# A hybrid decoder step on one core: the first norm's squares on ScalarE with a fixed order of additions, and the gMLP masks applied in the rotation tables' buffers

## The chip, the core and the metric

The kernel runs on one NeuronCore of a Trainium2 chip. The core has TensorE (PE in the profile: matrix products from SBUF into PSUM), VectorE (DVE), ScalarE (ACT), GpSimd (POOL) and SyncE (SP, which here only issues DMAs). Each engine works through its own queue in order and waits on semaphores for the others. The metric is the device time of one execution in microseconds; lower is better.

## What is computed

One step of a two-layer decoder for a prompt of 512 tokens and for 64 sample tokens (8 sequences of 8), 576 columns in all, width 1024, in float32. Layer 0 runs retention heads beside a gMLP, layer 1 a sliding-window attention; each is followed by a squared-ReLU MLP. The change is in the first norm and in the gMLP's masks of layer 0:

```python
def rmsnorm(x, g):
    x32 = x.astype(jnp.float32)
    y = x32 * lax.rsqrt(jnp.mean(x32 * x32, axis=-1, keepdims=True) + RMS_EPS)
    return (y * g.astype(jnp.float32)).astype(x.dtype)
...
def mixer_ab(h, pos, s0, w_in, w_s, b_s, ln_g, ln_b, w_o):
    z = h @ w_in
    q, k, v, g, u, gv = jnp.split(z, AB_SPLITS, axis=-1)
    q = rotary(q.reshape(B, L, RET_HEADS, RET_DK), pos)
    k = rotary(k.reshape(B, L, RET_HEADS, RET_DK), pos)
    o, s_new = retention(q, k, v, s0.astype(jnp.float32))
...
    causal = jnp.tril(jnp.ones((GM_CHUNK, GM_CHUNK), dtype=bool))
    w = jnp.where(causal[None], w_s, 0.0).astype(vn.dtype)
    mixed = jnp.einsum('gij,bnjgd->bnigd', w, vc) + b_s.T.astype(vn.dtype)[None, None, :, :, None]
```

`hn = rmsnorm(h, norm_mix[0])` feeds `mixer_ab`; the outputs are both residual streams after the last norm, the retention states, the normalised gMLP rows and the key and value caches.

## The kernel before

**Layout.** Activations lie transposed: eight chunks `h[0..7]` of 128 channels x 576 tokens. A float32 product is made of three fp32r products: an operand x is split into `hi` (rounded to fp32r) and `lo` (the rest), and `block` (line 330) adds hi·hi, hi·lo and lo·hi, in two halves of 288 columns, in PSUM. One chunk of the input projection is thus 8 x 6 = 48 products into an accumulator `acc` (two of them in PSUM). Weights come by DMA into `raw` (three buffers), `whi` is cast on ACT (L278), `wlo` subtracted on DVE (L289), each in a ring of six buffers.

**The norm comes late.** `operands(c)` multiplies h[c] by the gain only: `xhi` on ACT, `xlo` on DVE (L426). The factor rstd (one over the root mean square of a token) is applied to the products when they leave PSUM. So the projection starts before the norm is known. Squares are taken on ACT (L435) or POOL (L433), added on POOL (L441) into `ssq`; `two_parts` (L393) splits ssq, and `mean_rsqrt` (L398) multiplies it by a matrix of 1/1024 on PE (L404, L405), which sums over the channels, then takes a root on ACT (L406) and one Newton step on DVE (L407, L389 to L391).

**The start of `mixer0`** (line 698). For each chunk c: operands, a square, every second time the split of a 256-column piece of weights (`whf`, `wlf`, L227), then 12 products: v of head 0 and k of head 0 grow together in both accumulators, while h still arrives. Then `v1`, the product for v of head 1, in two small PSUM banks (`m_tile`, a ring of four), with the norm's products among it. Then `v_out(0)` frees the first accumulator (`vz`, L809), the rotation tables `cosr` and `sinr` are multiplied by rstd, and `k_out`, `q_out` rotate (`rotary`, line 784: three products on DVE, L786 to L788, and a sum on POOL, L789). Each result is passed on in later slots: `to_tokens` transposes on PE into m_tiles (`tp`, `tq`), `tokens` copies them (ACT) and makes `v2h`, `v2l` (L823) and the masked `vm` (POOL, L827); `scores` multiplies `sc`, `kv`, `scs` and `cx` (L872 to L882), all in m_tiles.

**The gMLP's masks.** The matrices `wst` (128 x 512) and `ws8` (64 x 256) are loaded and multiplied by a triangle on POOL (L1037, L1039) in the code behind the first gv chunk; they are read in `spatial` (L990, L992), after the second gate chunk. Their buffers are their own; cosr and sinr take two of the 21 buffers of the ring `w`.

**Order.** DVE and ACT run as written from line 730 to line 1011, and again in the last chunk and the MLPs (`manual_schedule`). Elsewhere, and on PE, POOL and SP everywhere, a scheduler orders the instructions by its own estimates when the kernel is built; so POOL took up the masks long ahead of their place in the code.

## Time and profile before

| | |
|---|---|
| median of 3 runs | 1206.8 us (1206.55 to 1207.28) |
| the profiled execution's own time | 1204.73 us |
| its span | 1202.9 us |
| instructions on DVE, ACT, POOL | 1691, 1111, 130 |
| share of DVE, ACT, POOL in the span | 76%, 49%, 12% |
| moved by DMA | 109.43 MB, mean 91 GB/s |

The span is the time from the first to the last instruction that the profiler saw; the execution's own time is a little longer. A row of the profile names the line of the code, the engine, the operation, what is written and read (`out<-in`, buffer numbers left out), and how often. In rows in order of time the first two numbers are the start and the length in microseconds (several alike in a row are merged, x2), and a bracket at the end tells how long the engine had been idle before and whom it waited for. DMA issues are SPq.

### The profile page before, as it was taken

To read this page: it belongs to the slowest core of one execution; us is meant where nothing else is said; L and a number is where in the kernel's file an instruction comes from. 1 tells how busy PE (TensorE), PEld (TensorE's weight loads), DVE (VectorE), ACT (ScalarE), POOL (GpSimd) and SP (SyncE) were. 2 spreads that over 40 slices of the span, in tenths; PEclk is the share of its full clock that TensorE was granted. 3 is DMA by queue.
4 is the path that set the end of the run, shared out by engine and by line. 5 is a ranking of instruction groups with operands and counts; after the bars stand their busy time and mean duration, and the time that the engine had idled before them with its cause. 6 is when DMAs were issued, how large, how long until landed. Compare 5 with 4: busy or idle time off the path is not lost.

```text
span 1202.9 us, 22619 instructions
## 1 busy us (share of the span) xinstructions
PE 1182.9 (98%) x9130; PEld 1164.8 (97%) x9130; DVE 908.2 (76%) x1691; ACT 588.4 (49%) x1111; POOL 148.3 (12%) x130
## 2 busy tenths in 40 slices
PE   8999999999999999999999999999999999999996
PEld 8899999999999999999999998999999999999996
DVE  8977797987866876885797787546785795795696
ACT  6333554654534444443466877445453453453452
POOL 4444250000000000000002653220000000000000
PEclk9999999999999999999999999999999999999999
DMA  7343222322332232242223211122233233233322
GB/s 269 110 142 112 88 65 80 88 81 78 90 106 87 77 117 71 71 120 75 88 87 111 72 53 55 53 76 71 84 105 89 71 106 91 68 106 88 87 73 79
DMA packets 38264, 109.43 MB, mean 91 GB/s; under 512 B 4160, under 2 KB 12544, under 8 KB 38144
## 3 DMA queue, kind: packets, MB, share of 16 engines
q1 hardware_dynamic: 37440, 107.36, 29.1%
q8 instruction: 72, 1.18, 0.4%
q10 hardware_dynamic: 720, 0.62, 0.2%
q14 instruction: 32, 0.26, 0.1%
HBM read 102.92 MB, written 6.03 MB: 91 GB/s over the span
## 4 chain that ended last, share of the span: by engine, by line
PE 82%; DVE 10%; ACT 4%; DMA 3%; issue 1%; SPq 0%; DVEq 0%; ACTq 0%
PE acc L334 50%; PE acc L346 10%; PE y L346 4%; PE f L346 4%; PE w L346 3%; PE z L346 3%; DVE wlo L289 3%; DMA raw<-in_w_dn 2%; ACT s L1158 1%; DVE alo L505 1%; PE tpp L1218 1%; DVE h L557 1%; ACT ahi L504 1%; PE dn L334 1%; PE op L1233 1%
## 5 line engine op out<-in xcount | busy, mean ns | idle before, releaser
L334 PE MATMUL acc<-xhi,whi 128*128 128x288 f32 x1504 | 321.7, 295 | 0.3 <-DVE vz L809 0.3
L334 PE MATMUL acc<-xhi,wlo 128*128 128x288 f32 x1504 | 319.2, 293 | 0.0
L334 PE MATMUL acc<-xlo,whi 128*128 128x288 f32 x1504 | 318.6, 293 | 0.0
L289 DVE TENSOR_TENSOR wlo<-raw,whi 128x512 fp32r<-128x512 f32 x317 | 235.7, 757 | 68.8 <-ACT whi L278 67.5
L334 PEld LDWEIGHTS acc<-xhi,whi 128*128 128x128 f32 x1504 | 239.5, 188 | 1.6 <-issue 1.1
L334 PEld LDWEIGHTS acc<-xhi,wlo 128*128 128x128 f32 x1504 | 240.5, 188 | 0.3
L334 PEld LDWEIGHTS acc<-xlo,whi 128*128 128x128 f32 x1504 | 240.1, 188 | 0.0
L278 ACT CAST whi<-raw 128x512 fp32r<-128x512 f32 x317 | 188.9, 619 | 100.5 <-PE acc L334 73.3
L501 ACT ACTIVATE q<-t 128x576 f32<-128x576 f32 x64 | 44.0, 687 | 227.8 <-DVE t L496 227.8
L278 ACT CAST whi<-s 128x512 fp32r<-128x512 f32 x140 | 83.4, 621 | 72.4 <-DVE s L263 62.8
L496 DVE SCALAR_TENSOR_TENSOR t<-acc,rstd 128x576 f32<-128x576 f32 x64 | 48.3, 755 | 80.6 <-PE acc L334 80.4
L289 DVE TENSOR_TENSOR wlo<-s,whi 128x512 fp32r<-128x512 f32 x140 | 95.9, 697 | 10.8 <-ACT whi L278 10.8
L505 DVE TENSOR_TENSOR alo<-q,ahi 128x864 fp32r<-128x864 f32 x64 | 77.2, 1205 | 8.3 <-ACT ahi L504 8.3
L504 ACT CAST ahi<-q 128x864 fp32r<-128x864 f32 x64 | 66.6, 1041 | 13.5 <-DVE q L536 12.5
L346 PE MATMUL acc<-ahi,wlo 128*128 128x288 f32 x340 | 71.4, 298 | 0.6
L346 PE MATMUL acc<-ahi,whi 128*128 128x288 f32 x340 | 71.4, 295 | 0.0
L346 PE MATMUL acc<-alo,whi 128*128 128x288 f32 x340 | 70.4, 295 | 0.0
L1102 POOL TENSOR_TENSOR kl<-z,kh 64x512 fp32r<-64x512 f32 x4 | 5.5, 1374 | 475.1 <-ACT kh L1099 474.9
L263 DVE TENSOR_TENSOR s<-raw 128x512 f32<-128x512 f32 x70 | 48.7, 695 | 19.8 <-DMA raw<-in_w_dn 19.8
L346 PEld LDWEIGHTS acc<-ahi,wlo 128*128 128x128 f32 x340 | 53.5, 188 | 2.5 <-DVE wlo L289 2.5
L346 PEld LDWEIGHTS acc<-ahi,whi 128*128 128x128 f32 x340 | 54.0, 188 | 0.0
L346 PEld LDWEIGHTS acc<-alo,whi 128*128 128x128 f32 x340 | 53.7, 188 | 0.0
(386 smaller groups left out, 2118.8 us busy)
## 6 DMA issues: line engine op xcount, KB each, us to landing
raw<-in_w_up SPq DMA_DIRECT2D x64, 512.0 KB
raw<-in_w_dn SPq DMA_DIRECT2D x64, 512.0 KB
raw<-in_w_in SPq DMA_DIRECT2D x22, 512.0 KB
raw<-in_w_o SPq DMA_DIRECT2D x16, 512.0 KB
raw<-in_w_qkv SPq DMA_DIRECT2D x10, 512.0 KB
h<-in_xT SPq DMA_DIRECT2D x8, 288.0 KB
s<-in_s SPq DMA_DIRECT2D x4, 512.0 KB
out_ret_s<-s SPq DMA_DIRECT2D x4, 512.0 KB
```

The costliest lines, as they stand in the source:

```text
L263: nc.vector.tensor_tensor(out=sums[k, i], in0=x, in1=b[y], op=ALU.add)
L278: nc.scalar.copy(out=hi, in_=src)
L289: nc.vector.tensor_tensor(out=lo, in0=src, in1=hi.bitcast(F32), op=ALU.subtract)
L334: nc.tensor.matmul(out, lhsT=w_, rhs=x_[:, hf if isinstance(hf, slice) else half(hf)], start=(start and si == 0), stop=(stop and si == 2))
L346: nc.tensor.matmul(out, lhsT=w[wi][:, k * P:(k + 1) * P], rhs=x(k)[xi], start=(start and n == 0), stop=(stop and n == len(steps) - 1), ski ...
L496: nc.vector.scalar_tensor_tensor(out=halves(t), in0=view, scalar=0.0, in1=norm.rv, op0=ALU.max, op1=ALU.mult)
L501: nc.scalar.activation(out=flat(q[:, seg]), in_=t, func=AF.Square)
L504: nc.scalar.copy(out=hi[:, s0 - 1:s1 - 1], in_=q[:, s0:s1])
L505: nc.vector.tensor_tensor(out=lo[:, s0 - 1:s1 - 1], in0=q[:, s0:s1], in1=hi.bitcast(F32)[:, s0 - 1:s1 - 1], op=ALU.subtract)
L557: nc.vector.tensor_tensor(out=row[:, cols_], in0=row[:, cols_], in1=src, op=op)
L1158: nc.scalar.activation(out=s[:, n, cut_:], in_=s[:, n, cut_:], func=AF.Exp, bias=nm[:, n:n + 1], accum_out=den[:, n:n + 1])
L1218: nc.tensor.transpose(out=tp[:, i * P:(i + 1) * P], in_=s[:, n, hf * P:(hf + 1) * P], identity=ident)
```

## The change

All eight squares of the first norm are taken on ACT. They are added on DVE in one chain of seven additions into the square of chunk 1, at places that the code writes down (`add`); DVE and ACT run in written order from the first chunk on. The sum isn't split any more: `finish(True)` multiplies it as float32 by `ones_d` (one product for each half instead of two). The split of the first weights is written in another order among this. `ones_v` and `eps_l` are made earlier. cosr and sinr get a pair of buffers of their own (`rot`), which wst and ws8 take over after the last rotation; the ring `w` shrinks from 21 to 19.

```diff
--- before.py
+++ after.py
@@ -35,7 +35,7 @@
 RMS_EPS = 1e-6
 LN_EPS = 1e-5
 MINF = -1e30
-NW = 21
+NW = 19
 NW1 = 26
 NSB = 4
 NK = 9
@@ -397,12 +397,14 @@
 
     def mean_rsqrt(ones_r, sq, out, temp, parts_=None):
 
-        hi, lo = parts_ or two_parts(sq, temp)
+
+        parts_ = parts_ or two_parts(sq, temp)
         r0, x = temp("rs0"), temp("rsx")
         for hf in range(2):
             ms = m_tile("ms")
-            nc.tensor.matmul(ms[:, 0:TH], lhsT=ones_r, rhs=hi[:, half(hf)], start=True, stop=False)
-            nc.tensor.matmul(ms[:, 0:TH], lhsT=ones_r, rhs=lo[:, half(hf)], start=False, stop=True)
+            for n, part in enumerate(parts_):
+                nc.tensor.matmul(ms[:, 0:TH], lhsT=ones_r, rhs=part[:, half(hf)], start=(n == 0),
+                                 stop=(n == len(parts_) - 1))
             nc.scalar.activation(out=r0[:, half(hf)], in_=ms[:, 0:TH], func=AF.Abs_reciprocal_sqrt, bias=eps_r)
             nc.vector.scalar_tensor_tensor(out=x[:, half(hf)], in0=ms[:, 0:TH], scalar=RMS_EPS, in1=r0[:, half(hf)],
                                            op0=ALU.add, op1=ALU.mult)
@@ -427,12 +429,9 @@
                                            op0=ALU.mult, op1=ALU.subtract)
             self.xs.append((hi, lo))
 
-        def square(self, c, pool=False, add=True, eng=None):
+        def square(self, c, add=True, eng=None):
             sq = ks("ssq" if c == 0 else "sq")
-            if pool:
-                nc.gpsimd.tensor_tensor(out=sq, in0=h[c], in1=h[c], op=ALU.mult)
-            else:
-                nc.scalar.activation(out=sq, in_=h[c], func=AF.Square)
+            nc.scalar.activation(out=sq, in_=h[c], func=AF.Square)
             if not add:
                 return sq
             if c == 0:
@@ -440,9 +439,12 @@
             else:
                 (eng or nc.gpsimd).tensor_tensor(out=self.ssq, in0=self.ssq, in1=sq, op=ALU.add)
 
-        def finish(self, parts_=None):
+        def finish(self, plain=False):
             self.rstd = ks("rstd")
-            mean_rsqrt(ones_dr, self.ssq, self.rstd, ks, parts_)
+            if plain:
+                mean_rsqrt(ones_d, self.ssq, self.rstd, ks, [self.ssq])
+            else:
+                mean_rsqrt(ones_dr, self.ssq, self.rstd, ks)
             self.rv = halves(self.rstd)
 
     def add_residual(dc, view, bias=None):
@@ -707,35 +709,51 @@
                 off, wd = C0W[name]
                 return cst[:, off:off + wd]
 
+            ones_v = mp.tile([P, P], F32R, name="ones_v", bufs=1)
+            nc.gpsimd.tensor_scalar(out=ones_v, in0=ones_d, scalar1=float(D // P), scalar2=None, op0=ALU.mult)
+            eps_l = mp.tile([P, 1], F32, name="eps_l", bufs=1)
+            nc.gpsimd.memset(eps_l, LN_EPS)
+
 
             accs = [acc_tile() for _ in range(2)]
-            rest = []
+            inorder = tc.manual_schedule(engines={mybir.EngineType.DVE, mybir.EngineType.Activation})
+            inorder.__enter__()
+            squares = {}
+
+            def square(*chunks):
+                for c in chunks:
+                    squares[c] = norm.square(c, False)
+
+            def add(*chunks):
+                for c in chunks:
+                    nc.vector.tensor_tensor(out=squares[1], in0=squares[1], in1=squares[c], op=ALU.add)
+
             for c in range(KC):
                 norm.operands(c)
-                if c:
-                    rest.append(norm.square(c - 1, c in (1, 3), c <= 5))
+                if c in (4, 6):
+                    square(c - 2)
                 if c % 2 == 0:
                     hi = wp.tile([P, 512], F32R, name="whf", tag="whi", bufs=NW_)
                     lo = wp.tile([P, 512], F32R, name="wlf", tag="wlo", bufs=NW_)
                     split_into(first[c // 2], hi, lo)
+                if c in (1, 3, 5):
+                    square(c // 2 if c < 5 else 3)
+                add(*{4: [0], 5: [2], 6: [3]}.get(c, []))
                 for j in range(2):
                     ws = slice((c % 2) * 256 + j * P, (c % 2) * 256 + (j + 1) * P)
                     block([accs[j][:, hf, 0:TH] for hf in range(2)], (hi[:, ws], lo[:, ws]), norm.xs[c], (0, 1),
                           c == 0, c == KC - 1)
-            sq5, sq6, sq7 = rest[-2], rest[-1], norm.square(KC - 1, False, False)
-            nc.vector.tensor_tensor(out=sq5, in0=sq5, in1=sq6, op=ALU.add)
-            nc.vector.tensor_tensor(out=sq5, in0=sq5, in1=sq7, op=ALU.add)
-
-            inorder = tc.manual_schedule(engines={mybir.EngineType.DVE, mybir.EngineType.Activation})
-            inorder.__enter__()
+            square(5)
+            add(4, 5)
+            split_to(1)
+            square(6, 7)
+            add(6, 7)
             split_to(2)
-            nc.vector.tensor_tensor(out=norm.ssq, in0=norm.ssq, in1=sq5, op=ALU.add)
-            ssq_parts = two_parts(norm.ssq, ks)
+            norm.ssq = squares[1]
 
             split_high(4)
-            split_low(2)
             xs = norm.xs
-            cosr, sinr = w("cosr"), w("sinr")
+            cosr, sinr = (wide.tile([P, T], F32, name=n, tag="rot", bufs=2) for n in ("cosr", "sinr"))
             nc.sync.dma_start(out=cosr, in_=a["rot"][0])
             nc.sync.dma_start(out=sinr, in_=a["rot"][1])
             cst = mp.tile([P, C0.shape[1]], F32, name="cst", bufs=1)
@@ -745,15 +763,12 @@
             used[0] += 2
             for k in range(KC):
                 if k == 2:
-                    norm.finish(ssq_parts)
+                    split_low(1)
+                    norm.finish(True)
                 block([t[:, 0:TH] for t in v1], cut(got, k), xs[k], (0, 1), k == 0, k == KC - 1)
             split_high(6)
             rv = norm.rv
 
-            ones_v = mp.tile([P, P], F32R, name="ones_v", bufs=1)
-            nc.gpsimd.tensor_scalar(out=ones_v, in0=ones_d, scalar1=float(D // P), scalar2=None, op0=ALU.mult)
-            eps_l = mp.tile([P, 1], F32, name="eps_l", bufs=1)
-            nc.gpsimd.memset(eps_l, LN_EPS)
             outs, acts, late = [None] * KC, [], [None]
 
             def keep_out(k, src):
@@ -1030,9 +1045,9 @@
                 chunk(xs, lambda v: gv_out(g, v))
                 if g == 0:
 
-                    wst = mp.tile([P, NH, P], F32, name="wst", bufs=1)
+                    wst, ws8 = (wide.tile([P, T], F32, name=n, tag="rot", bufs=2)[0:r, 0:NH * r].rearrange(
+                        "p (h i) -> p h i", h=NH) for n, r in (("wst", P), ("ws8", NS)))
                     nc.sync.dma_start(out=wst, in_=a["wst"])
-                    ws8 = mp.tile([NS, NH, NS], F32, name="ws8", bufs=1)
                     nc.sync.dma_start(out=ws8, in_=a["ws8"])
                     nc.gpsimd.tensor_tensor(out=wst, in0=wst, in1=con("tri")[:, None, :].broadcast_to([P, NH, P]),
                                             op=ALU.mult)
```

How this moves the instructions is read from the queues that the two builds leave. DVE, from the sixth chunk's split to the splits of the first full matrices (xlo is an operand's low half, wlf and wlo the weights', sq and ssq squares and their sum); before:

```order
L426 SCALAR_TENSOR_TENSOR xlo<-h_90,cols,xhi 128x576
L426 SCALAR_TENSOR_TENSOR xlo<-h_92,cols,xhi 128x576
L227 TENSOR_TENSOR wlf<-rawf,whf 128x512
L426 SCALAR_TENSOR_TENSOR xlo<-h_96,cols,xhi 128x576
L726 TENSOR_TENSOR sq<-sq 128x576
L727 TENSOR_TENSOR sq<-sq 128x576
L289 TENSOR_TENSOR wlo<-raw,whi 128x512 x2
L732 TENSOR_TENSOR ssq<-ssq,sq 128x576
L227 TENSOR_TENSOR sql<-ssq,sqh 128x576
L289 TENSOR_TENSOR wlo<-raw,whi 128x512 x2
```

and now:

```order
L729 TENSOR_TENSOR sq<-sq,ssq 128x576
L428 SCALAR_TENSOR_TENSOR xlo<-h_90,cols,xhi 128x576
L729 TENSOR_TENSOR sq<-sq 128x576
L428 SCALAR_TENSOR_TENSOR xlo<-h_92,cols,xhi 128x576
L227 TENSOR_TENSOR wlf<-rawf,whf 128x512
L729 TENSOR_TENSOR sq<-sq 128x576
L428 SCALAR_TENSOR_TENSOR xlo<-h_96,cols,xhi 128x576
L729 TENSOR_TENSOR sq<-sq 128x576 x2
L289 TENSOR_TENSOR wlo<-raw,whi 128x512
L729 TENSOR_TENSOR sq<-sq 128x576 x2
L289 TENSOR_TENSOR wlo<-raw,whi 128x512 x2
```

Three additions now stand ahead of the last xlo and four behind it; the split sql is gone, and one wlo fewer stands ahead of the norm's factor.

POOL, from the rotation of head 0's k to that of its q (`vm` masked values, `qd` the decayed q); before:

```order
L789 TENSOR_TENSOR kT<-t_412,t_413 128x576
L827 TENSOR_TENSOR vm_503<-v2h,cst 128x1024
L1037 TENSOR_TENSOR wst<-wst,cst 128x512
L1039 TENSOR_TENSOR ws_1498<-ws_1498,cst 64x256
L789 TENSOR_TENSOR qT<-t_477,t_478 128x576
L827 TENSOR_TENSOR vm_505<-v2l,cst 128x1024
L859 TENSOR_TENSOR qd<-qT,cst 128x512
L862 TENSOR_TENSOR qd<-qT,cst 128x64
```

and now:

```order
L804 TENSOR_TENSOR kT<-t_405,t_406 128x576
L842 TENSOR_TENSOR vm_494<-v2h,cst 128x1024
L804 TENSOR_TENSOR qT<-t_468,t_469 128x576
L842 TENSOR_TENSOR vm_496<-v2l,cst 128x1024
L874 TENSOR_TENSOR qd<-qT,cst 128x512
L877 TENSOR_TENSOR qd<-qT,cst 128x64
```

The two mask products have left this place; they now stand behind the qd of head 3.

SP, the loads behind the constants `cst` (`raw` are weight matrices, s_ the states of heads 0 and 1, `rows` the layer norm's gains and the gMLP's biases); before:

```order
L742 DMA cst<-in_c 128x1776
L235 DMA raw<-in_w_in 128x1024 x3
L854 DMA s_474<-in_s 128x1024
L854 DMA s_700<-in_s 128x1024
L235 DMA raw<-in_w_in 128x1024
L1024 DMA rows<-in_rows 128x1536
L1034 DMA wst<-in_wst 128x512
L1036 DMA ws_1498<-in_ws 64x256
L235 DMA raw<-in_w_in 128x1024
```

and now:

```order
L760 DMA cst<-in_c 128x1776
L235 DMA raw<-in_w_in 128x1024 x2
L869 DMA s_465<-in_s 128x1024
L869 DMA s_694<-in_s 128x1024
L1039 DMA rows<-in_rows 128x1536
L235 DMA raw<-in_w_in 128x1024
L1085 DMA out_ck_s<-in_cache_k 8x15360
L235 DMA raw<-in_w_in 128x1024
```

Both states and `rows` have moved ahead of the fifth matrix, and the masks' loads have left for a place behind head 3's rotation.

## The prediction

> **What bounds the kernel now.** I read the page's head and busy line first, then TensorE's waits over the whole span, longest first, then busy time by stretches of the first microseconds, and last the sum of such stretches from 60 to 240 us.
>
> ```profile
> span 1202.9 us, 22619 instructions
> PE 1182.9 (98%) x9130; PEld 1164.8 (97%) x9130; DVE 908.2 (76%) x1691; ACT 588.4 (49%) x1111; POOL 148.3 (12%) x130
> ...
> PE kv L875 <- DVE v2l L823: 2.1, 1, 2.1
> ...
> PE acc L334 <- DVE xlo L426: 0.8, 3, 0.3
> ...
> 10.00:20.00 10.00, 8.72 (x58) 7.55 (x57) 10.00 (x8) 7.28 (x13) 7.41 (x8) 1.00 0.78 259
> ...
> 40.00:50.00 10.00, 7.90 (x72) 7.36 (x72) 9.91 (x9) 3.55 (x9) 6.71 (x6) 1.00 0.11 45
> ...
> sum 180.00, PE 179.72 PEld 175.90 DVE 150.05 ACT 86.46 POOL 52.03; mean PE 9.98 PEld 9.77 DVE 8.34 ACT 4.80 POOL 2.89
> ```
>
> TensorE (PE) is busy for 98% of the span. A stretch row gives length, then busy time of PE, PEld, DVE, ACT, POOL, the clock, the DMA share and GB/s. From 60 to 240 us PE is idle for 0.28 us of 180, so there an edit of another engine gains nothing by itself; but whatever PE gains earlier is handed on to the end, since all that follows hangs on PE. The idle time is in the first 50 us: in the start, where DVE is busy for 10.00 of 10 us with 8 instructions (more than a microsecond each), and at the kv products of head 0. The whole question is how much of these the change returns.
>
> **The start.** These rows are PE's first product, its first product of the second stage (v1) and the first that needs the factor rstd; then DVE, POOL and ACT in the same time.
>
> ```profile
> 5.38 0.83 PE L334 MATMUL acc<-xhi,whf 128*128 128x288 f32 x2
> ...
> 21.70 0.42 PE L334 MATMUL v<-xhi,whi 128*128 128x288 f32 x2
> ...
> 25.17 0.43 PE L334 MATMUL v<-xhi,whi 128*128 128x288 f32 x2
> ...
> 28.90 0.42 PE L334 MATMUL v<-xhi,wlo 128*128 128x288 f32 x2
> ...
> 29.64 0.50 PE L334 MATMUL acc<-xhi,whi 128*128 128x288 f32 x2 [0.32 <-DVE vz L809]
> ...
> 14.39 3.89 DVE L426 SCALAR_TENSOR_TENSOR xlo<-h,cols,xhi 128x576 fp32r<-128x576 f32 x2
> ...
> 18.20 0.68 DVE L227 TENSOR_TENSOR wlf<-rawf,whf 128x512 fp32r<-128x512 f32 x1
> ...
> 18.80 0.81 DVE L426 SCALAR_TENSOR_TENSOR xlo<-h,cols,xhi 128x576 fp32r<-128x576 f32 x1
> ...
> 19.53 0.75 DVE L726 TENSOR_TENSOR sq<-sq 128x576 f32<-128x576 f32 x1
> ...
> 13.99 3.66 POOL L441 TENSOR_TENSOR ssq<-ssq,sq 128x576 f32<-128x576 f32 x2
> ...
> 10.81 0.61 ACT L226 CAST whf<-rawf 128x512 fp32r<-128x512 f32 x1
> ...
> 14.32 0.78 ACT L425 ACTIVATE xhi<-h,cols 128x576 fp32r<-128x576 f32 x1
> ```
>
> While POOL runs two additions (13.99 to 17.65), two xlo take DVE 3.89 us. When POOL is done, one takes 0.81, and rows follow one another 0.08 sooner than they end: a wlf takes 0.60 us (18.20 to 18.80), an xlo 0.73 (18.80 to 19.53), an addition then 0.67. So DVE and POOL hold each other up. PE takes 16.32 us (5.38 to 21.70) for 96 products that, at the pace of the v1 rows (28 from 25.17 to 28.90: 0.133 each), need 12.8: 3.5 us lost, waiting for xlo and wlf.
>
> The change takes six squares and additions from POOL here. ACT gains square 0 and keeps 1; square 2 takes the place of 3 and so on, so ACT has as many instructions between the fourth and the last xhi as before, and square 0 falls into a gap in which ACT waits for h. I therefore leave the ACT times: third whf done at 11.42, last xhi at 15.1. DVE gains three additions ahead of the last xlo. From 11.45 I step: wlf 0.60, add 0.67, xlo 0.73, add 0.67, xlo 0.73, wlf 0.60, add 0.67, xlo 0.73, together 5.4: the last xlo is done at 16.9, where it was 19.6. PE needs 12 x 0.133 = 1.6 us for a chunk; if it loses some 0.5 at the first one, it comes to the last at 5.4 + 0.5 + 7 x 1.6 = 17.1 and finds its xlo there. It gets to v1 at 5.4 + 12.8 + 0.5 = 18.7, not 21.70: **3.0 us**.
>
> **The norm.** The rows are the last sum, the low half of its split and the factor itself on DVE, then float32 products of the same form at the kernel's end.
>
> ```profile
> 22.25 0.75 DVE L732 TENSOR_TENSOR ssq<-ssq,sq 128x576 f32<-128x576 f32 x1
> ...
> 23.80 0.76 DVE L227 TENSOR_TENSOR sql<-ssq,sqh 128x576 fp32r<-128x576 f32 x1 [0.80 <-ACT sqh L226]
> ...
> 25.71 0.85 DVE L407 SCALAR_TENSOR_TENSOR rsx<-ms,rs 128x288 f32<-128x288 f32 x2
> ...
> 27.88 0.76 DVE L391 TENSOR_TENSOR rstd<-rsx,rs 128x576 f32<-128x576 f32 x1
> ...
> 1185.68 0.65 PE L650 MATMUL msf<-ssq,ones_d 128*128 128x288 f32 x2
> ...
> 1186.17 0.65 PE L651 MATMUL msf<-sqf,ones_d 128*128 128x288 f32 x2
> ```
>
> After the last xlo come four additions and one wlo: 16.9 + 4 x 0.67 + 0.60 = 20.2 (22.9 before). The split (sqh on ACT, 0.8 us of idle DVE, sql) goes. In its place PE multiplies ssq itself. A float32 product of this form is two records that start again after 0.49 us (1185.68, 1186.17); two halves take 0.97 us where four fp32r products took 4 x 0.133 = 0.53: PE pays 0.44 us. They stand behind 15 products of v1 (18.7 + 2.0 = 20.7), so PE doesn't wait for ssq, by a margin of 0.5. The second half is there at 21.7. The chain from rsx to rstd, 2.93 us (25.71 to 28.64) of the same instructions, begins with the first half's root, at about 22.0: rstd at 24.9, and vz of head 0, one DVE instruction later, frees the accumulator at 25.7. PE has finished v1 at 18.7 + 48 x 0.133 + 0.97 = 26.05, so the wait of 0.32 is gone, and the next product starts at 26.05 instead of 29.64: **3.6 us** in all so far. What is late next here is nothing but PE itself.
>
> **Head 0.** The rows are the products sc and kv on PE, then DVE and POOL ahead of them.
>
> ```profile
> 44.75 1.05 PE L872 MATMUL sc<-qT,kT 128*128 128x128 f32 x8
> ...
> 47.90 1.13 PE L875 MATMUL kv<-vt,kt 128*128 128x128 f32 x8 [2.10 <-DVE v2l L823]
> ...
> 39.04 0.58 DVE L823 TENSOR_TENSOR v2l<-tq,v2h 64x128 fp32r<-64x128 f32 x2
> ...
> 40.93 6.33 DVE L289 TENSOR_TENSOR wlo<-raw,whi 128x512 fp32r<-128x512 f32 x2
> ...
> 47.18 0.57 DVE L823 TENSOR_TENSOR v2l<-tq,v2h 64x128 fp32r<-64x128 f32 x2
> ...
> 37.63 1.90 POOL L827 TENSOR_TENSOR vm<-v2h,cst 128x1024 fp32r<-128x1024 f32 x1 [1.37 <-ACT v2h L821]
> 39.49 1.29 POOL L1037 TENSOR_TENSOR wst<-wst,cst 128x512 f32<-128x512 f32 x1
> 40.72 0.79 POOL L1039 TENSOR_TENSOR ws<-ws,cst 64x256 f32<-64x256 f32 x1
> 41.48 1.42 POOL L789 TENSOR_TENSOR qT<-t,t 128x576 f32<-128x576 f32 x1
> 42.87 1.89 POOL L827 TENSOR_TENSOR vm<-v2l,cst 128x1024 fp32r<-128x1024 f32 x1
> 44.72 1.26 POOL L859 TENSOR_TENSOR qd<-qT,cst 128x512 f32<-128x512 f32 x1
> ```
>
> Two wlo, 0.60 us each with POOL idle (a wlo has the form of wlf), take 6.33, as long as POOL runs without a gap (to 46.71 with a small last qd). v2l of head 1 stands behind them, and kv needs the PSUM buffer that v2l reads: 2.10 us lost. The change moves the two mask products, 39.49 to 41.48, out of this run: the run is 2.0 us shorter. Its start depends on the rotation of q0, which DVE now begins one wlo later (about 0.7 us later against PE; the order below). So POOL ends at 46.71 - 3.6 - 2.0 + 0.3 = 41.4, v2l at about 42.8, and PE comes to kv at about 42.6 (it also waits some 0.6 us longer for v2l of head 0 at the transposes). Kv starts at 42.8 instead of 47.90: **5.0 us** in all; a wait of 0.2 is left. Bounds: if the 2.1 us stay whole, 3.6 - 0.6 = 3.0; if both waits go, 3.6 + 2.1 + 0.3 = 6.0. I take 5.0, as the rows of POOL name the length of the run.
>
> The Trainium skill, "SBUF — State Buffer", section "Who interferes with whom", says that a VectorE instruction with two SBUF inputs and a GpSimd one that reads SBUF exclude each other, whichever came first holding the shared port pair for its whole instruction. The trace agrees in kind: v2l, with one input in PSUM, keeps 0.29 us each at 39.04, while POOL runs vm and the first mask. It disagrees on the end of the wait: the rule would let the first wlo in after one GpSimd instruction, while the rows show it held over qT, vm and qd. By the rule alone the two mask products would cost less here, and what is left would be smaller.
>
> **The masks' new place.** Their buffers are free after head 3's last rotation.
>
> ```profile
> 115.72 0.75 DVE L788 TENSOR_TENSOR t<-acc,sinr 64x576 f32<-64x576 f32 x1
> ...
> 109.59 15.58 SPq L235 DMA_DIRECT2D raw<-in_w_in  x4
> ...
> 162.49 0.89 PE mx L990 x8
> ```
>
> That is at 116.5 - 5 = 111.5. The transfer lands a few us on, the two products (1.29 + 0.79) run on POOL by about 118, and mx reads them at 162.5 - 5. The SP queue holds loads behind this wait, but the four of 109 to 125 are of matrices that the order of the weights puts three or more chunks of 48 x 0.133 = 6.4 us behind this rotation. DVE may be held for 2 us; two accumulators give it the 6.4 us of a chunk. Cost: nothing, 2 us at the worst. The w ring of 19 instead of 21 loses only the two that cosr and sinr held; after 116 it is smaller by two, and the only wait added there is of DVE for itself: nothing.
>
> **The sum.** Profiled execution 1204.73 us (span 1202.9 and 1.8 around it) less 5.0 is 1199.7; that execution is 2.1 below the median of the runs, 1206.8, so against the median 1201.8.
>
> **Rivals.** (1) *The kv wait stays.* The order puts s0, s0 and rows (512 + 512 + 768 KB) ahead of the fifth weight matrix. With a full DMA (259 / 0.78 = 332 GB/s in the stretch of 10 to 20) they take 5.5 us: asked for at some 21, they are through near 28, and the matrix at about 30, my estimate. ACT casts its second half here:
>
> ```profile
> 36.05 0.62 ACT L278 CAST whi<-raw 128x512 fp32r<-128x512 f32 x1 [2.58 <-PE acc L334]
> ```
>
> That is at 32.4 in the new time, with head 0's copies behind it. If the matrix lands after that, kv is late by as much; with 2 us the gain is 3.0, 1203.8. For it speaks the DMA share of 0.78; against it that this cast waited for PE, not for a load. (2) *The port frees after one instruction.* The first wlo would then wait for qT at most (1.42) and kv for nothing: gain 6.0, 1200.8; against it stands the row of 6.33. This is what the rule of the Trainium skill above would give. (3) *Off the path.* Something that I take as ready, the h loads or the roots, sets the start: gain 1 to 2, 1205.3. (4) *Slower.* The long rows of DVE are not POOL's doing but the instruction's own wait for data. Then three additions push the last xlo from 19.6 to 21.6, v1 to 23.7, its end with the float32 products to 31.1: 1.5 us later than 29.64, and the later rotation adds 0.7: 1209.0, or 1209.5 if ssq is late too. It decides as soon as xlo keeps over 1.3 us with POOL idle; the rows of 18.20 and 18.80 speak against it.
>
> **How the numbers follow.** Forecast (gain 3.6 to 5.7) 0.60, rival 1 0.16, rival 2 0.08, rival 3 0.10, rival 4 0.06. A measurement tells 0.2%, 2.4 us, from no change. Faster: the first three, 0.84, less 0.03 for the low edge of rival 1, is 0.81; slower by over 2.4 us: a third of rival 4 and some for the unseen, 0.03; within: 0.16. The range takes the forecast, rivals 1 and 2 with 0.6 us for the spread of runs: 1200.2 to 1204.4.
>
> **What would show it.** Right: the xlo of 14.39 at 0.8 us each, v1 at about 18.7, the first product after the norm near 26, kv near 42.8 with a wait under 0.5, and no new PE wait after 60. Wrong: a DVE row over 1.3 us in the first 20; a wait of ACT's whi for a load; a kv wait of 2; waits near 115.

## The result, and the profile after

| | median us | lowest to highest | runs |
|---|---|---|---|
| before | 1207.04 | 1206.55 to 1208.85 | 4 |
| after | 1199.65 | 1198.75 to 1200.73 | 4 |

The ratio is 0.9943 (95%: 0.993 to 0.9955), a gain of 6.9 us (5.4 to 8.4); the two medians are 7.4 us apart. The forecast was 5.0 and 1201.8; the time is 0.55 us below the low end of the range, 1200.2. With all timed runs taken together, 63 of the kernel before have a median of 1205.82 and a mean of 1205.86, 16 of the one after a median of 1198.91 and a mean of 1199.25: a gain of 6.9 by medians and 6.6 by means. The profiled execution of after took 1200.73 us, the slowest of its four.

The head and busy line of the page of after:

```profile
span 1198.8 us, 22608 instructions
PE 1182.2 (99%) x9130; PEld 1165.7 (97%) x9130; DVE 902.0 (75%) x1694; ACT 586.7 (49%) x1112; POOL 139.9 (12%) x124
```

TensorE's waits in after, with the releaser, the sum, the number of times and the longest; then busy time by stretches (columns as in the prediction), the last row a sum over 60 to 240 us (its means are of stretches of 20 us, those in the prediction of 10, so only the sums compare):

```profile
PE z L346 <- DVE wlo L289: 1.6, 4, 0.7
...
PE tq L811 <- DVE v2l L838: 0.6, 1, 0.6
```

```profile
10.00:20.00 10.00, 10.00 (x77) 10.00 (x76) 9.53 (x14) 8.52 (x15) 0.00 (x0) 1.00 0.97 354
...
40.00:50.00 10.00, 10.00 (x90) 9.61 (x90) 6.35 (x13) 0.37 (x1) 3.35 (x3) 1.00 0.11 24
...
sum 180.00, PE 179.67 PEld 175.93 DVE 154.84 ACT 88.48 POOL 49.57; mean PE 19.96 PEld 19.55 DVE 17.20 ACT 9.83 POOL 5.51
```

The kv wait of 2.1 us is gone from the list, and a wait of 0.6 at tq is new, as the prediction had it for the transposes. The z row, 0.4 us in before, is now 1.6, all of it behind 860 us; in two more executions of the same kernel (d1 and d5 below) it is 0.6 and 0.4, so the growth belongs to this execution. PE is busy for 10.00 of 10 us in both stretches that had holes. In the first one DVE now runs 14 instructions in 9.53 us, where it ran 8 in 10.00, and POOL none.

The timeline of after at the places of the prediction's steps: PE, then DVE, POOL and ACT (start, duration, engine, line, operation, and in brackets the idle time before it and what ended it):

```profile
18.86 0.43 PE L334 MATMUL v<-xhi,whi 128*128 128x288 f32 x2
...
20.87 1.13 PE L406 MATMUL ms<-sq,ones_d 128*128 128x288 f32 x4
...
26.12 0.49 PE L334 MATMUL acc<-xhi,whi 128*128 128x288 f32 x2
...
42.57 1.06 PE L890 MATMUL kv<-vt,kt 128*128 128x128 f32 x8
43.56 0.33 PE L892 MATMUL scs<-qT,kT 128*64 128x64 f32 x2
43.81 0.64 PE L897 MATMUL cx<-s,qd 128*32 128x128 f32 x16
...
12.35 0.81 DVE L428 SCALAR_TENSOR_TENSOR xlo<-h,cols,xhi 128x576 fp32r<-128x576 f32 x1
...
24.34 0.76 DVE L391 TENSOR_TENSOR rstd<-rsx,rs 128x576 f32<-128x576 f32 x1
...
37.73 4.00 DVE L289 TENSOR_TENSOR wlo<-raw,whi 128x512 fp32r<-128x512 f32 x2
41.65 0.57 DVE L838 TENSOR_TENSOR v2l<-tq,v2h 64x128 fp32r<-64x128 f32 x2
...
37.53 1.95 POOL L842 TENSOR_TENSOR vm<-v2l,cst 128x1024 fp32r<-128x1024 f32 x1
39.44 1.74 POOL L874 TENSOR_TENSOR qd<-qT,cst 128x512 f32<-128x512 f32 x1
...
30.62 0.62 ACT L278 CAST whi<-raw 128x512 fp32r<-128x512 f32 x1 [3.94 <-DMA raw<-in_w_in]
32.56 0.62 ACT L278 CAST whi<-raw 128x512 fp32r<-128x512 f32 x1 [1.32 <-PE acc L334]
```

xlo takes 0.81 where pairs took 3.89. v1 begins at 18.86 (forecast 18.7), the float32 product at 20.87 (20.7), rstd is through at 25.1 (24.9), the first product after the norm begins at 26.12 (26.05), kv at 42.57 (42.8), with no wait. Each step of the start came out within 0.25 us. So the prediction lost its 2 us somewhere else: behind kv, or in the number that the sum was made against.

To find the place, the k-th product of each kind was matched in two traces and its start compared. Against the profile on which the prediction was made, PE in after is ahead by:

```
          at 60 us   170    700    790    900   1160
after       5.40    5.88   5.87   5.98   4.84   3.62
before, a second execution (d2_before_again): behind by
            1.45    1.45   1.57   2.97   3.98   4.42
```

The lead is made in the first 50 us, grows by 0.48 until 170 us, and part of it is given back from 800 us on (1.0 at 820 to 860 us by PE's pace, told in the last section, and 1.2 later, as much as the z waits have grown). But the second execution of the kernel before gives back more: its time is 1209.16, that of the first was 1204.73. The execution that the sum was made against was a quick one, and the first 1.45 us by which the second falls behind it lie in head 0, in the place that the change is about.

### The profile page after: what moved, and what is told of

Read it like the earlier page. It is cut to its first block, busy times and chain, and to the rows that moved or that the text cites. A ratio compares the mean times of both kernels' runs of the same rounds, so it can differ in the third digit from the quotient of the medians.

```text
span 1198.8 us, 22608 instructions
## 1 busy us (share of the span) xinstructions
PE 1182.2 (99%) x9130; PEld 1165.7 (97%) x9130; DVE 902.0 (75%) x1694; ACT 586.7 (49%) x1112; POOL 139.9 (12%) x124
## 4 chain that ended last, share of the span: by engine, by line
PE 84%; DVE 9%; ACT 3%; DMA 2%; issue 1%; DVEq 0%; ACTq 0%; SPq 0%
PE acc L334 52%; PE acc L346 10%; PE w L346 3%; PE f L346 3%; PE y L346 3%; PE z L346 3%; DMA raw<-in_w_dn 2%; DVE wlo L289 2%; ACT s L1173 1%; DVE alo L507 1%; PE tpp L1233 1%; PE op L1248 1%; PE v L334 1%; ACT ahi L506 1%; DVE h L559 1%
## 5 line engine op out<-in xcount | busy, mean ns | idle before, releaser
L289 DVE TENSOR_TENSOR wlo<-raw,whi 128x512 fp32r<-128x512 f32 x317 | 229.6, 738 | 66.8 <-ACT whi L278 65.6
```

What stands on the lines that cost most here:

```text
L289: nc.vector.tensor_tensor(out=lo, in0=src, in1=hi.bitcast(F32), op=ALU.subtract)
```

## The experiments

### Each half of the change alone, and both kernels again

e1_masks_only is the kernel before with the masks' buffers of the kernel after:

```
-NW = 21
+NW = 19
-            cosr, sinr = w("cosr"), w("sinr")
+            cosr, sinr = (wide.tile([P, T], F32, name=n, tag="rot", bufs=2) for n in ("cosr", "sinr"))
-                    wst = mp.tile([P, NH, P], F32, name="wst", bufs=1)
+                    wst, ws8 = (wide.tile([P, T], F32, name=n, tag="rot", bufs=2)[0:r, 0:NH * r].rearrange(
+                        "p (h i) -> p h i", h=NH) for n, r in (("wst", P), ("ws8", NS)))
-                    ws8 = mp.tile([NS, NH, NS], F32, name="ws8", bufs=1)
```

> The kernel of before with the masks alone moved into the rotation tables' buffers (ring w 19). Run theory (the length of GpSimd's unbroken run decides): the start is as before (v1 at 21.7, the first product after the norm at 29.6 us), the run at head 0 is 2.0 us shorter, kv starts at about 45.9 instead of 47.90 with a wait under 0.3, and the kernel gains 2.0 us, ratio 0.9983. Rival, the port frees after one instruction: the masks held VectorE for one instruction only, kv at 47.2 or later, gain 0 to 0.7 us.

The timeline of e1 at head 0, POOL, DVE and PE:

```profile
37.59 1.90 POOL L827 TENSOR_TENSOR vm<-v2h,cst 128x1024 fp32r<-128x1024 f32 x1 [1.35 <-ACT v2h L821]
39.45 1.42 POOL L789 TENSOR_TENSOR qT<-t,t 128x576 f32<-128x576 f32 x1
...
41.02 3.99 DVE L289 TENSOR_TENSOR wlo<-raw,whi 128x512 fp32r<-128x512 f32 x2
...
45.66 1.13 PE L875 MATMUL kv<-vt,kt 128*128 128x128 f32 x8
```

qT follows vm at once, since the two masks are gone from POOL's run. The held pair takes 3.99 instead of 6.33, and kv begins at 45.66 without a wait instead of 47.90: 2.24 us. 1202.89 us, ratio 0.9978 (0.9969 to 0.9988). The forecast's 2.0 for a run shorter by the two products holds; kv at 47.2 or later, the rival's, did not come.

How the pair is let in is another matter, and the merged rows (x2) hide it. The first wlo of the pair alone, in before and in after:

```profile
40.93 5.60 DVE L289 TENSOR_TENSOR wlo<-raw,whi 128x512 fp32r<-128x512 f32 x1
...
37.73 2.29 DVE L289 TENSOR_TENSOR wlo<-raw,whi 128x512 fp32r<-128x512 f32 x1
```

In before it is passed over when POOL goes on to qT (41.48), to vm (42.87) and to qd (44.72), and is through at 46.54, beside the small last qd. In after it is through at 40.03, 0.6 us after POOL went from vm to qd (39.44), and the second one, of 1.78, as long after POOL's next change (41.14); qd takes 1.74 there and 1.26 in before. e1 is like after (2.29 and 1.77). So with the masks the first wlo was held over the run, and without them each of the two waited for one POOL instruction. In all of them the pair ends within 0.6 us of POOL's run.

e2_squares_only is the other half: the edit above undone in the kernel after (NW 21, cosr and sinr from the w ring, wst and ws8 in buffers of their own).

> The changed kernel with the masks where they were (own buffers, ring w 21), so the squares, the additions and the float32 product alone. Run theory: v1 at 18.9, first product after the norm at 26.1, then the kv wait of head 0 is still there, 1.5 to 2.2 us, and kv starts at about 44.5; gain 3.4 us, ratio 0.9972. Rival, the gain of the change lies in the start alone: kv at 42.6 as in the changed kernel, gain 5.4 us or more, ratio 0.9955 or less.

The timeline of e2, POOL and PE:

```profile
33.22 1.73 POOL L1052 TENSOR_TENSOR wst<-wst,cst 128x512 f32<-128x512 f32 x1
34.92 1.18 POOL L1054 TENSOR_TENSOR ws<-ws,cst 64x256 f32<-64x256 f32 x1
...
38.38 0.30 PE L811 MATMUL tq<-ident,vz 128*64 128x128 f32 x1 [1.81 <-DVE v2l L838]
...
44.81 1.13 PE L890 MATMUL kv<-vt,kt 128*128 128x128 f32 x8 [0.45 <-DVE v2l L838]
```

POOL now takes the masks ahead of vm, so v2l of head 0 is late too: the 2.10 at kv became 1.81 at tq and 0.45 at kv. PE is 3.09 us ahead at 60 us; the squares alone are worth 3.1 there, the masks alone 2.25 (e1), together 5.34 against the 5.40 of the whole change. 1200.83 us, ratio 0.9961 (0.9947 to 0.9976). By their times the halves are worth more than at 60 us of one trace: 2.7 us for the masks (1.4 to 3.7) and 4.7 for the squares (2.9 to 6.4), though both intervals reach down to the trace's.

d1_after_again and d2_before_again are the two kernels unaltered.

> The changed kernel once more, unaltered. Theory A (what differs after 800 us is of the execution, not of the change): TensorE stands 5.9 us ahead of the first profile of before at 800 us, within 0.2, and at another distance than 3.6 us at the end; ratio 0.994 to 0.9955. Rival B (the change costs 2 us in the second MLP): again 3.6 us at the end, given back at the same places (820 to 860, 965, 1055, 1150 us).

> The kernel of before once more, unaltered, against itself: ratio 1.000 within 0.001. Theory A: TensorE is within 0.3 us of the first profile of before up to 800 us, and up to 2 us later at the end, since that first profile (1204.73) was 2 us faster than the median. Rival B: within 0.3 us to the end.

d1: 1199.24 us, ratio 0.9947 (0.9932 to 0.9961). PE is ahead by 5.30 at 60 us, but by 4.2 at 800 and 3.2 at the end, which neither of its two theories had: near 750 us it loses 1.5 us more than the first profiles (the second place of the half clock, below). d2: 1205.12, ratio 0.9996 (0.9986 to 1.0007); its 1.45 us at 60 us are in neither theory either. The timeline of d2 behind kv; then, from busy time by stretches, the 3.4 us behind the start of kv in d2, and under it the same stretch of the first profile of before (the clock is the third number from the end):

```profile
47.85 2.01 PE L875 MATMUL kv<-vt,kt 128*128 128x128 f32 x8 [2.08 <-DVE v2l L823]
49.79 0.48 PE L877 MATMUL scs<-qT,kT 128*64 128x64 f32 x2
50.19 1.08 PE L882 MATMUL cx<-s,qd 128*32 128x128 f32 x16
```

```profile
47.90:51.30 3.40, 3.40 (x27) 2.64 (x27) 3.34 (x6) 0.00 (x0) 0.59 (x1) 0.50 0.00 0
```

```profile
47.90:51.30 3.40, 3.40 (x37) 3.01 (x38) 3.34 (x6) 0.37 (x1) 0.54 (x1) 1.00 0.00 0
```

The wait is the same (2.08 and 2.10), but in d2 PE's clock is granted at 0.50 for 3.4 us behind it: kv takes 2.01 where it took 1.13, and PE makes 27 products in the stretch where it made 37. This costs 1.45 us, and it was not in the profile that the sum was made from.

### The half clock and the wait

e6_masks_twice, the kernel before with POOL's run made longer:

```
                     nc.gpsimd.tensor_tensor(out=ws8, in0=ws8,
                                             in1=con("tris")[0:NS, None, :].broadcast_to([NS, NH, NS]), op=ALU.mult)
+                    nc.gpsimd.tensor_tensor(out=wst, in0=wst, in1=con("tri")[:, None, :].broadcast_to([P, NH, P]),
+                                            op=ALU.mult)
+                    nc.gpsimd.tensor_tensor(out=ws8, in0=ws8,
+                                            in1=con("tris")[0:NS, None, :].broadcast_to([NS, NH, NS]), op=ALU.mult)
```

> The kernel before, with its two mask products on POOL at head 0 made twice (the second time by the same factors of 0 and 1, which change nothing). Theory of the run (the wlo of VectorE is held until POOL's whole run is through): the run is longer by 1.29 + 0.79 = 2.0 us, the held wlo pair takes about 8.3 instead of 6.33, and PE's wait at kv is about 4.1 instead of 2.1. Rule of the skill's page (the port goes over after one instruction): the pair is let in between, and the wait grows by less than 1. New theory on why the medians gained more than the profile on which the sum was made: PE's granted clock falls to half for 3.4 us after this wait, in some executions of the kernel before (second look: 0.50 from 47.9 to 51.3, and 1.45 us lost there) and not in others (first profile). A wait of 4.1 us, longer than that stretch, should be followed by half clock in nearly every execution: this profile shows 0.5 for about 3.4 us from 50 on, and the time is 2.0 us plus up to 1 us above the kernel before. Rival (the half clock at 48 us was an accident that has nothing to do with the wait): clock 1.00 behind kv, and 2.0 us above the kernel before.

The timeline of e6 (DVE, PE), and its stretch behind kv:

```profile
40.94 8.22 DVE L289 TENSOR_TENSOR wlo<-raw,whi 128x512 fp32r<-128x512 f32 x2
...
49.81 2.04 PE L875 MATMUL kv<-vt,kt 128*128 128x128 f32 x8 [3.98 <-DVE v2l L823]
```

```profile
49.00:56.00 7.00, 6.19 (x37) 5.46 (x38) 6.29 (x14) 0.37 (x1) 1.41 (x1) 0.53 0.00 0
```

The pair is held 1.9 us longer, as long as POOL's run, and the wait is 3.98. The clock behind it is 0.5, for two stretches of 3.4 us. At 60 us PE is 4.77 behind the first profile: 1.9 of longer wait and 2.9 of half clock. 1209.18 us, ratio 1.0026 (1.0015 to 1.0038): 3.1 us for 2.0 us of work, and five of its six runs have a mean clock of 0.993 or 0.994.

d3_before_look and d4_before_look, the kernel before twice more:

> The kernel before, unaltered, one more look, for one thing: whether the half clock behind the kv products of head 0 is there. So far it is in one look of two. Theory: it comes in about half or more of the executions, since it depends on how the wait of 2.1 us lies against windows of 3.4 us; then kv takes 2.0 us instead of 1.13, and all behind it is 1.45 us late. Rival: the one look was a rare accident, and kv takes 1.13.

> The same as the run before it, a second look: half clock behind kv or not. If neither of the two shows it, the half clock at head 0 explains little of the difference between the medians, and the prediction's missing 2 us stay open.

The timeline of d3 behind kv:

```profile
47.76 1.13 PE L875 MATMUL kv<-vt,kt 128*128 128x128 f32 x8 [2.09 <-DVE v2l L823]
48.82 0.33 PE L877 MATMUL scs<-qT,kT 128*64 128x64 f32 x2
49.08 1.08 PE L882 MATMUL cx<-s,qd 128*32 128x128 f32 x16
```

d3 has it, a little later (cx takes 1.08, not 0.64; 1.37 us lost at 60 us, not by kv as expected); d4 has not, and is 0.03 from the first profile there. So two profiled executions of four of the kernel before have it, and none of the nine of kernels without a kv wait of 2 us (after, d1 and d5; e1, e2, e3, e4, e5 and e7).

d5_after_third, the kernel after once more:

> The changed kernel once more, unaltered, beside the run above. By my theory of the gain (5.9 us at the same granted clock, and the half clock behind kv that only the kernel before has): 1198.2 to 1200.7, 5.9 to 7.4 under the kernel before in the same job, clock 1.00 at 40 to 55 us in its profile. By the prediction as put down: 5.0 under it.

1198.40 us, ratio 0.9943 (0.9927 to 0.9958), 5.1 to 8.8 us under the kernel before: the 5.0 lies just outside, as in the first comparison; in d1's, 4.7 to 8.2, it lies inside. The two profiled executions without any half clock before the end of PE's work, d4 (1203.19) and d5 (1197.65), are 5.5 us apart.

### POOL and VectorE in the start

e4_pool_reads and e5_pool_writes put work of POOL's back into the start of the kernel after; nothing reads it. In the loop over the chunks of h:

```
 e4: +                if c in (0, 2, 3, 4, 5, 6):
     +                    nc.gpsimd.tensor_tensor(out=junk, in0=h[c], in1=h[c], op=ALU.mult)
 e5: +                if c in (0, 2, 3, 4, 5, 6):
     +                    for _ in range(3):
     +                        nc.gpsimd.memset(junk, float(c))
```

> The changed kernel, with six products h[c] times h[c] on POOL (128x576, float32, into a buffer that nothing reads) as the pieces of h arrive, so that POOL reads SBUF through the first 20 us again; no other instruction depends on them. The prediction's step for the start (POOL's reading instructions and VectorE's with two SBUF inputs hold each other up): xlo, wlf and the additions that fall beside POOL's rows take 1.3 us and more instead of 0.7 to 0.8, and v1 begins 1 to 3 us later than 18.86. Its rival 4 (the long rows of the kernel before were those instructions' own waits for data, and the gain of the start came from something else): every row keeps 0.7 to 0.8 us and v1 begins at 18.7 to 19.1.

> The changed kernel with POOL busy in the same stretch with instructions that only write SBUF: 18 memsets of a 128x576 float32 buffer that nothing reads. The Trainium skill, SBUF - State Buffer, section Who interferes with whom, says that a VectorE instruction with two SBUF inputs contends with a GpSimd instruction that reads SBUF and not with one that only writes it. By that rule, and by the port theory of the start as I hold it: rows of 0.7 to 0.8 us on VectorE and v1 at 18.7 to 19.1. Rival (any work of POOL's on SBUF stretches VectorE): rows of 1.2 us and more beside POOL's, and v1 0.5 to 3 us later.

The timeline of e4, DVE, POOL and PE:

```profile
11.89 3.32 DVE L428 SCALAR_TENSOR_TENSOR xlo<-h,cols,xhi 128x576 fp32r<-128x576 f32 x2
15.13 0.68 DVE L227 TENSOR_TENSOR wlf<-rawf,whf 128x512 fp32r<-128x512 f32 x1
...
6.70 7.89 POOL L744 TENSOR_TENSOR junk<-h 128x576 f32<-128x576 f32 x5
...
22.09 0.42 PE L334 MATMUL v<-xhi,whi 128*128 128x288 f32 x2
```

And that of e5:

```profile
12.54 0.81 DVE L428 SCALAR_TENSOR_TENSOR xlo<-h,cols,xhi 128x576 fp32r<-128x576 f32 x1
...
5.96 10.79 POOL L745 MEMSET junk<- 128x576 f32 x17
...
18.48 0.43 PE L334 MATMUL v<-xhi,whi 128*128 128x288 f32 x2
```

With POOL reading, xlo is back at 1.66 each until POOL ends at 14.6, and at 15.13 a wlf takes 0.68 again. v1 begins at 22.09, 3.2 us later (a little more than expected), and all behind it is 3.6 us late at 60 us; the one time is 1205.15. With POOL writing for 10.8 us, xlo takes 0.81, v1 begins at 18.48, and the one time is 1200.08. So it was POOL's reading that made the long rows; rival 4 falls. The rule of the Trainium skill, "SBUF — State Buffer", section "Who interferes with whom", that an instruction which only writes does not contend, agrees with e5's rows.

### The float32 product

e3_split_sum, the kernel after with the sum split in two parts again:

```
-                mean_rsqrt(ones_d, self.ssq, self.rstd, ks, [self.ssq])
+                mean_rsqrt(ones_dr, self.ssq, self.rstd, ks, plain)
+            ssq_parts = two_parts(norm.ssq, ks)
-                    norm.finish(True)
+                    norm.finish(ssq_parts)
```

> The changed kernel with one part undone: the sum of the squares is split again into two fp32r parts (sqh by ScalarE, sql by VectorE) and TensorE makes four fp32r products of it instead of four float32 records. My theory (the float32 product costs PE 0.4 us and takes 0.8 us of split out of the chain to rstd): PE comes to the products at 20.9 as in the changed kernel's profile, but sqh is ready only near 20.8 and sql near 21.7, so PE or rstd is later: rstd's row begins at about 25.1 instead of 24.34, and the first product after the norm at 26.4 to 26.9 instead of 26.12; from 60 us on everything is 0.3 to 0.8 us later than in the changed kernel, and the time is 0.3 to 0.8 us above it. Rival (the split was hidden and the change paid 0.4 us for nothing): the first product after the norm at about 25.7, 0.4 us sooner than in the changed kernel. Either way the DVE rows of the start and the kv products of head 0 keep their places but for that shift.

The timeline of e3, DVE and PE:

```profile
21.62 0.76 DVE L227 TENSOR_TENSOR sql<-sq,sqh 128x576 fp32r<-128x576 f32 x1 [0.19 <-ACT sqh L226]
...
25.69 0.76 DVE L391 TENSOR_TENSOR rstd<-rsx,rs 128x576 f32<-128x576 f32 x1
...
27.46 0.50 PE L334 MATMUL acc<-xhi,whi 128*128 128x288 f32 x2 [1.25 <-DVE vz L825]
```

rstd begins 1.35 us later, and PE waits 1.25 for vz: 1.0 us lost at 60 us, more than the 0.3 to 0.8 expected, and on the side of my theory. Its 1199.65 us (ratio 0.9953, 0.994 to 0.9967) don't show that loss against the kernel after, whose three medians are 1198.40 to 1199.65: e3's profile has no half clock before the end, and the mean clock of four of its five runs is 0.997 or 0.998. A difference of 1 us is read from the matched products here, not from the times.

### The second place of the half clock

In several profiles the clock also falls to half near 750 us, behind 64 small products of the second mixer. e7_spread_samples, the kernel after with ordinary products between them:

```
-            def sample_values():
+            def sample_values(dense):
                 for b in range(DB):
+                    if b in dense:
+                        dense[b]()
...
-            part(0, 0, [5])
-            part(1, 0, [5])
-            sample_transpose()
-            part(0, 0, [6])
-            part(1, 0, [6])
-            sample_values()
+            with tc.manual_schedule(engines={mybir.EngineType.PE}):
+                sample_transpose()
+                part(0, 0, [5])
+                part(1, 0, [5])
+                sample_values({3: lambda: part(0, 0, [6]), 6: lambda: part(1, 0, [6])})
```

> The changed kernel, and beside the change: in the second mixer the 64 small products opS (128x64 and 64x64 wide, 4.2 us in one run at 747.2 of the changed kernel's profile) are parted by two blocks of three ordinary products (part of the output product, made 1 us later for it). In five of the seven looks with a profile so far at the kernel before and its variants' common program, TensorE's granted clock fell to half for 3.4 or 6.8 us at the end of that run (750 to 764), in three it did not. If it is that run of small products that brings the half clock, as the wait at kv brought it at head 0, then here the clock stays at 1.00 at 745 to 765, nearly all runs have a mean clock of 0.997 or 0.998, and the time is 1198.0 to 1198.8, some 1 us under the changed kernel's median in the same job. Rival (0.8 us of ordinary products doesn't matter to it, or the half clock has another cause): 0.5 at 750 as often as in the changed kernel, the same median within 0.5 us, or 0.5 us more for waits at pTS.

The counts in that text are wrong: seven of the ten profiles until then show this half clock (the first of each kernel, d1, d2, e2, e4, e5), three do not (e1, e3, e6). The timeline of e7, then the stretch in e7, and the same of after:

```profile
744.86 0.30 PE L1302 MATMUL tpS<-ident,sS 128*128 128x128 f32 x1 [1.03 <-DVE den L1178]
```

```profile
745.00:755.00 10.00, 10.00 (x121) 8.14 (x121) 3.95 (x11) 3.83 (x16) 3.62 (x4) 1.00 0.01 2
```

```profile
745.00:755.00 10.00, 9.82 (x99) 8.07 (x99) 4.39 (x13) 4.36 (x18) 3.65 (x4) 0.83 0.01 2
```

The clock stays at 1.00, and all six runs have a mean of 0.997 or 0.998 (1198.38 to 1199.53); of d5's six, taken beside them, three have less (1197.61 to 1199.97). But the new order brought a wait of 1.03 at the transposes, and the median, 1198.86, is not below d5's 1198.40. Since d3, d4 and d5 don't show this half clock either, the cause is supported, not shown, and no version beats the kernel after.

## Why the prediction's steps were right, and why its sum was too small

- **The start, 3.0 us:** right. v1 at 18.86 for 18.7; e4 takes 3.2 of it away by giving POOL reading work, e5 none by giving it writing work.
- **The norm, 3.6 in all:** right, 3.52 (29.64 to 26.12). Going without the split is worth 1.0 us at 60 us (e3), with the 0.44 us that the float32 product costs PE already paid.
- **Head 0, 5.0 in all:** right in size, 5.33 at kv (42.57 for 42.8), and right that the masks cost 2 us there: with them the pair follows the length of POOL's run, 6.33, and 8.22 with the masks twice. The way to 42.8 was only half right. The prediction let the pair in when POOL was through, near 41.4, and had v2l end at 42.8, a little too late for kv. In after each wlo waited for one POOL instruction, the pair was through at 41.73 with POOL busy until 41.91, v2l at 42.2, and kv waits for nothing. That the 5.0 came so close is in part luck.
- **Rivals 2 and 1:** that kv would wait for nothing is what rival 2 said. Its rule fails at the row of 6.33 and fits the rows of after, so neither account covers both kernels. Its gain of 6.0 left out the 0.6 at the transposes, which came (0.57); the 0.3 in it has no source in the prediction, for the vz wait of 0.32 is already in the 3.6. Of rival 1 the first half came true: the fifth matrix is late (the ACT row of 30.62, 3.94 us of waiting for a load, which the prediction had named as a sign of being wrong). But the next cast, at 32.56, waits 1.32 us for PE, so the load had some 1.3 us to spare.
- **The masks' new place:** right, the sum over 60 to 240 has lost 0.05 us of PE's busy time, no wait stands near 115, and the two products run on POOL from 115.17 to 117.85, by the 118 of the prediction.
- **The sum, the step that failed:** it took 5.0 us off one execution and set the median a fixed 2.1 us above that. The term that was mis-sized is the kv wait. It was priced at its 2.1 us, as the first profile shows it. In two profiled executions of four it costs 1.4 us more, since PE's clock is half behind it; the change takes that away too. How often this happens in the timed runs is not shown, since each lists only its mean clock: 57 runs of before have a mean of 0.9955, 16 of after 0.9961. The difference of 0.0006 (standard error 0.0003) of 1203 us is 0.7 us, as much as half of 1.4. Among runs of one mean clock the kernels are 5.4 to 5.9 us apart (0.997: 1203.69 over nine runs and 1198.03 over seven; 0.996: 1205.42 over 23 and 1199.53 over four; 0.995: 1206.42 over 16 and 1200.98 over four).
- **The rest of the 5.4 to 5.9.** 0.33 is kv's own, and 0.48 comes between 60 and 170 us, where no wait stands: in the kernels with the new squares (after, d1, d5, e2, e3, e4, e5, e7) and in none of the others. It comes from PE's pace, told below. The prediction put this at nothing, since it counted only PE's idle time there.
- **The step to the median:** "that execution is 2.1 below the median of the runs" carried the difference over as if it were noise that both kernels share. In part it was the half clock. For the rest the median of three runs was itself 0.9 above the mean of 63. So of the 7.15 between 1206.8 and 1199.65, 5.0 were forecast, 0.4 to 0.9 are size at one clock, some 0.7 the half clock, and 0.5 (0.9 of before, less 0.4 of after) the spread of small samples. The range reached down to a gain of 6.0 (rival 2) and 0.6 us for the spread, which is too little for the last two.

## What to carry to other kernels

A wait of PE that one profile shows may cost more than its length in other executions: where the runs stand above the profiled execution, profile a second one and read the granted clock behind the wait before you add up. A VectorE instruction with two SBUF inputs can be held by a whole run of GpSimd's reading instructions, so count the run, and read the held instructions one by one, since a merged row doesn't show which of them was let in early; where GpSimd only wrote, it cost nothing (e5). Differences of 1 us in a kernel of 1200 are read from the products' starts in two traces, not from medians that the clock moves by more.

## What the hardware showed beside this

**The clock falls after short waits.** A wait of 2.08 to 2.10 us was followed by half clock in two executions of four, for 3.4 us, and one of 3.98 for 6.8. The Trainium skill, "TensorE: Matmul & The Clock Gate", section "Part 1: The HAM clock gate (the "warmup" mystery)", has windows of 3413 ns that run free of the program; the length of 3.4 and its double agree, and windows that lie differently in each execution would explain why the same wait has it or not. It names an idle window of about 3.4 us as the condition; here less was enough. The clock records of the traces bear the windows out: in each trace the changes of the clock lie whole steps of 3.413 us apart, so the steps can be counted back to kv. In d2 the wait (45.77 to 47.85) lies within one step (44.49 to 47.90), and in d3 too (45.67 to 47.76 in 45.67 to 49.08); the half clock begins where the step ends. In the first profile and in d4 a step ends inside the wait (at 47.65 and 47.34) and parts it into 1.85 and 0.25 us, and 1.5 and 0.6: no half clock. So 2.08 us of idle PE within one step had it and 1.85 had not. This was read afterwards; no run tested it.

**POOL and VectorE take turns in some places and not in others.** In e4 one instruction of each followed the other, and both were slower: xlo 1.66 instead of 0.81, POOL's products mostly 1.5 (7.89 for five, with gaps) where the first, beside a wlf that waited, took 1.27. At head 0 of after they take turns too (wlo 2.29 and 1.78, POOL's qd 1.74). At head 0 of before POOL kept its time, vm taking 1.89 beside the held pair and 1.90 before it (42.87 and 37.63 in the rows of the prediction), and the first wlo came in only with the run's last instruction. In e2, where the masks stand ahead of vm, another VectorE instruction (k, L862) was held for 4.62 us over qT, vm and both qd. What decides it wasn't tried.

**PE has two paces at the same clock.** Rows of the same kind of chunk in head 1, before and then after:

```profile
88.17 0.42 PE L334 MATMUL acc<-xlo,whi 128*128 128x288 f32 x2
...
89.76 0.43 PE L334 MATMUL acc<-xlo,whi 128*128 128x288 f32 x2
```

```profile
87.17 0.42 PE L334 MATMUL acc<-xhi,whi 128*128 128x288 f32 x2
...
88.47 0.42 PE L334 MATMUL acc<-xhi,wlo 128*128 128x288 f32 x2
```

12 products in 1.59 us are 0.1325 each, 10 in 1.30 are 0.130, with the clock at 1.00 in both. Stretches of some 6 to 40 us go at the one or the other pace, and which one differs between kernels and between executions: from 820 to 850 us it is 130.0 ns in the first profile of before and in d4, and 133.2 to 133.4 in d2, after and d5. That is the 0.48 us of the heads, and the 1.0 that after gives back at 820 to 860. What sets it stays open.
